# Down products of a macaron encoder as 2x2x2 block products, with the residual kept in DRAM meanwhile

## The chip, the core and the metric

The kernel runs on one core of a Trainium2 chip. The core has engines that work side by side, each on its own instructions in order: PE multiplies matrices (it loads a 128x128 weight block, then streams columns past it), DVE and ACT work on rows of 128 partitions, POOL does simple row operations and issues transfers of its own, SP only issues transfers. 16 DMA engines move the data that SP and POOL ask for. Only POOL's transfers can add to what lies at the destination. An engine waits for another on semaphores; an instruction that waits holds up all behind it on its engine.

The metric is the device time of one execution, in microseconds (us), as a median of several.

## The reference

Two layers on 528 tokens (16 meta tokens ahead of 512 frames) with 1024 features. Each layer has a feed-forward network (FFN), a mixer (attention beside a convolution), and a second FFN; so there are four FFNs. All values are float32.

```python
def swiglu(x, w_gate, w_up, w_down):
    return (jax.nn.silu(x @ w_gate) * (x @ w_up)) @ w_down
...
    for l in range(DEPTH):
        h = h + 0.5 * swiglu(rmsnorm(h, ffn1_norm[l]), ffn1_w_gate[l], ffn1_w_up[l], ffn1_w_down[l])
        h = h + hybrid_mixer(rmsnorm(h, mix_norm[l]), w_in[l], w_attn_out[l], conv_w[l], conv_b[l],
                             conv_ln_g[l], conv_ln_b[l], w_conv_out[l], w_out[l])
        h = h + 0.5 * swiglu(rmsnorm(h, ffn2_norm[l]), ffn2_w_gate[l], ffn2_w_up[l], ffn2_w_down[l])
    h = rmsnorm(h, final_norm)
    return h[:, N_META:]
```

The hidden width is 2816, which is 22 row tiles of 128. The last FFN works on the 512 frames alone.

## The kernel before

Features lie on partitions, tokens along the row: `h[0..7]` are eight tiles of 128 x 528. A float32 product is made of three products of rounded parts: each operand x is split into `hi`, a rounded copy (ACT, L79), and `lo`, the remainder (DVE, L80), and hi·hi, hi·lo and lo·hi are added up. So each weight tile and each activation passes ACT and DVE once before PE can use it.

**Weights** come in units, in the order of a list (L131 to 155). `unit` (L243) hands out the next one and prepares three units ahead: a raw tile `wr` (three buffers, loaded by SP at L191) is split into `wh` and `wl` (four buffers each). In the mixer DVE is spared: ACT writes the rounded copy and its negative (L224, L225), and a transfer from POOL adds the raw weight from DRAM to the latter (L226).

**Gate and up products** of two row tiles are made as one 2x2x2 block product in `quad` (L566): the depth is cut into two halves, the rows into two tiles, the tokens into two halves. Seven products of blocks stand for eight: four with weight blocks as they are (`w11`, `w22`, `w21` and, inside sums, `w12`), the others with sums of weight blocks, `s1` to `s4`. The sums `s1` and `s3` are made by transfers: SP loads one block, POOL adds a second from DRAM (`fetch_sums`, L196, L208 and L210, two buffers each); `s2` and `s4` follow from `s1` by a DVE addition (L236). The products run at L580 and are combined in PSUM by ACT copies and DVE operations (L599 to 613).

**Down products** (`down`, L622) run after each group of row tiles. The groups are

```python
GROUPS = ((0, 4), (4, 10), (10, 16), (16, 22))
```

For each of the eight output tiles j, in the order of `ORDER`, one unit of weights (`wr<-wd`, 384 KB for six row tiles) is multiplied with the group's split activations (L260): six row tiles x three products x two token halves, 36 matmuls of 264 columns, or 18 of 512 columns in the last FFN. For all but the last group, DVE scales the result by one half and by the norm factor (L638) into `dt`, and POOL adds that to `h[j]` in place (L640). The last group's result goes into `h[j]` directly (L633), and what the next part needs of `h[j]` is prepared there (`after`).

**Activations**: `parts` (L484) splits each row tile of silu(gate)·up into `ah` and `al`, six buffers each. `late` holds a row tile whose split is put into the next quad.

An FFN begins with plain rows (`head`, `first_head`): two row tiles, four in the first FFN, whose gate and up products are made without blocks while the sums are being built.

## Time and profile before

| what | us |
|---|---|
| median of 3 runs | 2152.22 |
| lowest, highest | 2151.51, 2152.39 |
| profiled execution: span from first to last instruction | 2150.5 |

No separate time of the profiled execution is at hand beyond its span; it lies 1.7 us under the median of the runs.

By windows of the trace, the four FFNs take 368.33, 357.56, 357.64 and 356.71 us, the two mixers 361.67 and 348.59 us.

How to read the profile's lines: a group line names the source line, the engine, the operation, what it writes and reads, and the count; then the busy time in us and the mean duration of one in ns; then the idle time of the engine before these instructions and what ended it. A line of windows gives, for a stretch in us from the start, its length, the busy time and number of instructions of each engine, PE's granted clock (1.00 is full), the share of time in which the DMA engines were taken, and what they moved in GB/s. A piece of the chain in order of time gives its start, its length, and the instructions in it. A line of a DMA queue gives packets, MB, and the time of the packets as a share of 16 engines; q1 holds SP's transfers, q0 those of POOL. A line of DMA issues ends with the size of one and the median time from issue to landing.

### The profile page before, as it was taken

Reading aid. Unit: us, or ns where it says so; the run is one execution under the profiler, and the core shown is the slowest. Engines: PE = TensorE matmul, PEld = TensorE weight load, DVE = VectorE, ACT = ScalarE, POOL = GpSimd, SP = SyncE. Lnnn points to the kernel's source line nnn. Section 1 sums busy time; section 2 is a strip of 40 time slices with the busy share of each in tenths; the row PEclk is TensorE's granted clock in tenths of the full one; section 3 lists DMA queues with packets and bytes.
Section 4 is the critical chain, followed back from the end, with each engine's and each line's share of the span. In section 5 each row is a group of like instructions: output and inputs, shape, how many; then the busy total and the mean of one; then the engine's idle time right before and its main releaser. Section 6 shows DMA issues by size and latency. Waiting matters only on the chain.

```text
span 2150.5 us, 39932 instructions
## 1 busy us (share of the span) xinstructions
PE 2135.9 (99%) x16226; PEld 2052.8 (95%) x16226; DVE 1521.5 (71%) x2091; ACT 1137.9 (53%) x1587; POOL 488.7 (23%) x449
## 2 busy tenths in 40 slices
PE   9999999999999999999999999999999999999998
PEld 9999999999999999999999999999888889999897
DVE  7867685677766777677877676856677767767685
ACT  6434355467776545343554443554778775444354
POOL 1322321211111131313113223212112111322320
PEclk9999999999999999999999999999999999999999
DMA  8465536865578747464365655368656886665542
GB/s 236 133 165 141 142 104 198 181 138 119 134 169 180 175 129 189 129 161 122 99 169 145 168 140 146 103 193 184 142 127 133 187 188 167 159 175 143 144 111 77
DMA packets 140168, 324.90 MB, mean 151 GB/s; under 512 B 15568, under 2 KB 19664, under 8 KB 139984
## 3 DMA queue, kind: packets, MB, share of 16 engines
q1 hardware_dynamic: 101856, 226.36, 33.3%
q0 software_dynamic: 37440, 95.44, 26.1%
q8 instruction: 127, 2.08, 0.4%
q10 hardware_dynamic: 688, 0.55, 0.1%
q14 instruction: 57, 0.47, 0.1%
HBM read 315.86 MB, written 6.42 MB: 150 GB/s over the span
## 4 chain that ended last, share of the span: by engine, by line
PE 99%; ACT 0%; DVE 0%; DMA 0%; issue 0%; DVEq 0%; ACTq 0%
PE pb L580 16%; PE ps L580 16%; PE ps L720 15%; PE ps L260 12%; PE ps L706 10%; PE pe L260 6%; PE pb L260 6%; PE pe L580 5%; PE z L706 2%; PE ps L502 2%; PE pe L502 1%; PE pb L502 1%; PE z L877 1%; PE po L921 1%; PE z L900 1%; PE ps L554 1%
## 5 line engine op out<-in xcount | busy, mean ns | idle before, releaser
L79 ACT CAST wh<-wr 128x1024 fp32r<-128x1024 f32 (+4 forms) x275 | 242.2, 887 | 372.4 <-PE ps L260 94.5
L80 DVE TENSOR_TENSOR wl<-wr,wh 128x1024 fp32r<-128x1024 f32 (+4 forms) x275 | 300.6, 1096 | 57.4 <-ACT wh L79 53.5
L79 ACT CAST wh<-s 128x1024 fp32r<-128x1024 f32 x158 | 165.8, 1049 | 274.9 <-DVE s L236 83.1
L80 DVE TENSOR_TENSOR wl<-s,wh 128x1024 fp32r<-128x1024 f32 x158 | 216.1, 1368 | 59.4 <-ACT wh L79 58.7
L720 PE MATMUL ps<-uh,wh 128*128 128x264 f32 (+1 forms) x792 | 243.8, 308 | 0.0
L720 PE MATMUL ps<-uh,wl 128*128 128x264 f32 (+1 forms) x792 | 240.0, 303 | 0.0
L720 PE MATMUL ps<-ul,wh 128*128 128x264 f32 (+1 forms) x792 | 239.9, 303 | 0.0
L640 POOL TENSOR_TENSOR h<-h,dt 128x528 f32<-128x528 f32 (+1 forms) x96 | 179.9, 1879 | 258.1 <-DVE dt L638 255.2
L210 POOL DMA_DIRECT2D s<-wg x78 | 72.8, 938 | 596.9 <-DMA s<-wg 337.9
L748 DVE SCALAR_TENSOR_TENSOR y<-uc,prm,y 128x528 f32<-128x528 f32 (+1 forms) x240 | 197.7, 824 | 4.1
L224 ACT CAST wh<-wr 128x1024 fp32r<-128x1024 f32 x104 | 109.1, 1049 | 141.2 <-issue 46.9
L580 PE MATMUL ps<-ul,wh 128*128 128x264 f32 (+1 forms) x624 | 177.4, 284 | 0.0
L580 PE MATMUL pb<-sl,wh 128*128 128x264 f32 (+1 forms) x624 | 176.9, 283 | 0.0
L580 PE MATMUL ps<-uh,wl 128*128 128x264 f32 (+1 forms) x624 | 176.9, 283 | 0.0
L580 PE MATMUL pb<-sh,wl 128*128 128x264 f32 (+1 forms) x624 | 176.8, 283 | 0.0
L580 PE MATMUL pb<-sh,wh 128*128 128x264 f32 (+1 forms) x624 | 176.5, 283 | 0.0
L580 PE MATMUL ps<-uh,wh 128*128 128x264 f32 (+1 forms) x624 | 176.2, 282 | 0.0
L720 PEld LDWEIGHTS ps<-uh,wl 128*128 128x128 f32 x792 | 149.1, 188 | 5.9
L720 PEld LDWEIGHTS ps<-uh,wh 128*128 128x128 f32 x792 | 148.9, 188 | 5.4
L720 PEld LDWEIGHTS ps<-ul,wh 128*128 128x128 f32 x792 | 149.0, 188 | 5.1
L260 PE MATMUL ps<-ah,wh 128*128 128x264 f32 (+1 forms) x616 | 142.0, 300 | 0.0
L260 PE MATMUL ps<-ah,wl 128*128 128x264 f32 (+1 forms) x616 | 141.8, 300 | 0.0
(319 smaller groups left out, 6460.8 us busy)
## 6 DMA issues: line engine op xcount, KB each, us to landing
wr<-wd SPq DMA_DIRECT2D x96, 384.0 KB, 3.6
wr<-win SPq DMA_DIRECT2D x72, 512.0 KB, 4.4
wl<-win POOLq DMA_DIRECT2D x72, 512.0 KB, 7.8
wr<-wg SPq DMA_DIRECT2D x117, 256.0 KB, 3.0
wr<-wu SPq DMA_DIRECT2D x117, 256.0 KB, 3.4
s<-wg SPq DMA_DIRECT2D x78, 256.0 KB, 5.2
s<-wu SPq DMA_DIRECT2D x78, 256.0 KB, 5.7
s<-wg POOLq DMA_DIRECT2D x78, 256.0 KB, 5.2
```

The costliest lines, as they stand in the source:

```text
L79: act.copy(hi, x)
L80: dve.tensor_tensor(out=lo, in0=x, in1=f(hi), op=ALU.subtract)
L210: pool.dma_start(t[:, a:b], src, accum_op=ALU.add)
L224: act.copy(hi[:, :nk], raw[:, :nk])
L260: pe.matmul(ps[:, c, :n], wt[:, k0 + k, :], xt[:, s:s + n], start=(k == 0 and pi == 0), stop=(k == end and pi == 2))
L502: pe.matmul(ps[:, e, :TH], wt[:, k, :], xt[:, s], start=(k == ORDER[0] and pi == 0), stop=(k == ORDER[-1] and pi == 2))
L554: pe.matmul(ps[:, e, :TH], wt[:, k, :], xt[:, s], start=(k == 0 and pi == 0), stop=(k == KD - 1 and pi == 2))
L580: pe.matmul(ps[:, e, :TH], wt[:, 4 * e + kk, :], xt, start=start and kk == 0 and pi == 0, stop=kk == 3 and pi == 2, skip_group_check=True)
L640: pool.tensor_tensor(out=tri(h[j], mode), in0=tri(h[j], mode), in1=tri(t, mode), op=ALU.add)
L706: pe.matmul(ps, wt[:, k0 + k, :], xt[:, s], start=(n == 0 and pi == 0), stop=(n == nk - 1 and pi == 2))
L720: pe.matmul(ps, wt[:, k, :], xt[:, s], start=(n == 0 and pi == 0), stop=(n == KD - 1 and pi == 2))
L748: t = dve.scalar_tensor_tensor(out=y, in0=uc[i][:, c0 + k:k + T], scalar=col(w0 + k), in1=y, op0=ALU.mult, op1=ALU.add)
```

## The change

Of the 22 row tiles of each FFN, the first 18 now go through block products in the down stage too. There are three groups of six row tiles and a last one of four, and the two row tiles of a quad are three apart, so that a group's first three tiles and last three are the two halves of the depth:

```diff
-GROUPS = ((0, 4), (4, 10), (10, 16), (16, 22))
-PLAIN, PLAIN_FIRST = 2, 4
+GROUPS = ((0, 6), (6, 12), (12, 18), (18, 22))
+NH = 3
+PAIRS = tuple(tuple((m0 + i, m0 + NH + i) for i in range(NH)) for m0, _ in GROUPS[:-1]) + (((18, 19), (20, 21)),)
+PLAIN, PLAIN_FIRST = 1, 2
...
+    DOWN = ((0, "w11"), (0, "w21"), (0, "s1"), (0, "s2"), (1, "w11"), (0, "s3"), (0, "w22"), (0, "s4"),
+            (1, "s1"), (1, "s2"), (1, "w21"), (1, "s3"), (1, "w22"), (1, "s4"))
```

A group's down stage is two block products, d = 0 and 1. Each makes four output tiles, two of the first four and two of the last four, for both token halves. Its seven units have 18 matmuls each, of 264 or 256 columns:

```diff
+            def down_quads(sp, gi):
+                item = late.pop()
+                sum_ops(dve, *item)
+                sum_parts(*item)
+
+                def products(ps, name, d, start=False):
+                    hi, lo = unit(name, fi, l, ("d", gi, d))
+                    for k in range(NH):
+                        xh, xl = a_parts[name, k]
+                        for pi, (wt, xt) in enumerate(((hi, xh), (hi, xl), (lo, xh))):
+                            for e in range(2):
+                                pe.matmul(ps[:, e, :TH], wt[:, NH * e + k, :], xt, start=start and k == 0 and pi == 0,
+                                          stop=k == NH - 1 and pi == 2, skip_group_check=True)
...
+                def give(src, c, t, d):
+
+                    dt = two(fp.tile([P, T], F32, tag="nt", bufs=3, name="dt"), mode)
+                    r = norm["r"][:, toks[t]].unsqueeze(1).to_broadcast([P, 2, TH])
+                    dve.scalar_tensor_tensor(out=dt, in0=src, scalar=0.5, in1=r, op0=ALU.mult, op1=ALU.mult)
+                    j = 4 * c + 2 * d
+                    pool.dma_start(residual[j:j + 2, :, toks[t]].rearrange("k p t -> p k t"), dt, accum_op=ALU.add)
...
+                A, B = begin_quad(0)
+                for d in range(2):
+                    if d == 0:
+                        products(A, "w21", 0)
+                        give(v(A), 0, 0, 0)
+                    G = ptile()
+                    products(G, "s1", d, True)
+                    q = sp.tile([P, 2, TH], F32, tag="q", bufs=2, name="q")
+                    act.copy(q, v(G))
+                    products(B, "s2", d)
+                    E = ptile("pe")
+                    dve.scalar_tensor_tensor(out=v(E), in0=v(B), scalar=-1.0, in1=q, op0=ALU.mult, op1=ALU.add)
+                    if d == 0:
+                        A = ptile()
+                        products(A, "w11", 1, True)
+                    else:
+                        products(A, "w21", 1)
+                        give(v(A), 0, 0, 1)
+                    products(B, "s3", d)
+                    c22 = sp.tile([P, 2, TH], F32, tag="c22", bufs=2, name="c22")
+                    dve.scalar_tensor_tensor(out=c22, in0=v(B), scalar=-1.0, in1=q, op0=ALU.mult, op1=ALU.add)
+                    products(E, "w22", d)
+                    give(c22, 1, 1, d)
+                    give(v(E), 1, 0, d)
+                    products(B, "s4", d)
+                    give(v(B), 0, 1, d)
+                    if d == 0:
+                        B = ptile("pb")
+                        act.copy(v(B), v(A))
```

The weights of these units: raw blocks `w11`, `w21`, `w22` of 384 KB, whose remainder is made in the way of the mixer, by a second ACT pass and an adding transfer from POOL; the sums `s1` and `s3` by transfers and `s2`, `s4` by DVE, as in a quad. The sums of the next block product are now asked for at its predecessor's `s1`, not at `w11`:

```diff
-            if nk == "w11":
+            if nk == "s1":
                 fetch_sums()
...
+            if is_down(n) and nk in RAW_OF:
+                act.copy(hi[:, :size], raw)
+                act.activation(lo[:, :size], raw, AF.Copy, scale=-1.0)
+                for a, b, src in pieces(n):
+                    pool.dma_start(into(lo, n, a, b), src.bitcast(F32R), accum_op=ALU.add)
+            else:
+                split(raw, hi[:, :size], lo[:, :size])
```

The activations need sums and differences of blocks too, and room for all their parts. Each pair of row tiles now has three and a half split rows in place of two. The four half-width operations that make the sums run on POOL inside the next quad, and for the last pair of a group on DVE ahead of the down stage:

```diff
+            def sum_ops(eng, p, ua, ub):
+
+                t1, t2 = toks
+                for o, x, y, op in ((ub[:, t2], ua[:, t2], ub[:, t2], ALU.subtract),
+                                    (ua[:, t2], ua[:, t1], ua[:, t2], ALU.subtract),
+                                    (ua[:, t1], ub[:, t2], ua[:, t1], ALU.subtract),
+                                    (ub[:, t1], ub[:, t1], ua[:, t1], ALU.add)):
+                    eng.tensor_tensor(out=o, in0=x, in1=y, op=op)
```

For that room `h` leaves the core: `leave` writes it to a DRAM tensor `hd` early in the FFN (SP, eight transfers of 264 KB), the freed tiles take activations (`slot`), `give` adds each result to `hd` by a transfer from POOL, and `back` loads `h` again ahead of the last quad.

```diff
+            def leave():
+
+                for k in ORDER:
+                    nc.sync.dma_start(tri(residual[k], mode), tri(h[k], mode))
+
+            def back():
+
+                for k in ORDER:
+                    h[k] = hpool.tile([P, T], F32, tag=f"h{k}", bufs=1, name=f"h{k}")
+                    nc.sync.dma_start(tri(h[k], mode), tri(residual[k], mode))
```

The order of instructions on two engines shows what moves. First POOL, in the first FFN. Before, this is what stands there around the down stage of the second group: the sums of the next quad, then the eight additions into `h`, then again sums.

```order
L210 DMA s3_2077<-wg1 128x512
L210 DMA s3_2077<-wu1 128x512
L210 DMA s1_2072<-wg1 128x512
L210 DMA s1_2072<-wu1 128x512
L640 TENSOR_TENSOR h0_77<-h0_77,dt_1922 128x528
L640 TENSOR_TENSOR h4_81<-h4_81,dt_1925 128x528
L640 TENSOR_TENSOR h1_78<-h1_78,dt_1972 128x528
L640 TENSOR_TENSOR h5_82<-h5_82,dt_2019 128x528
```

Now, in the same group's down stage, only transfers stand there: remainders of raw blocks (`wl<-wd`, L263), additions into the residual (`hd<-dt`, L747), and the next quad's sums (`s1`, `s3`, L230).

```order
L263 DMA wl_2303<-wd1 128x2x384
L747 DMA hd_134<-dt_2327 128x2x264
L263 DMA wl_2356<-wd1 128x2x384
L230 DMA s3_2416<-wg1 128x512
L230 DMA s3_2416<-wu1 128x512
L230 DMA s1_2411<-wg1 128x512
L230 DMA s1_2411<-wu1 128x512
L747 DMA hd_134<-dt_2466 128x2x264
L747 DMA hd_134<-dt_2469 128x2x264
L263 DMA wl_2473<-wd1 128x2x384
L747 DMA hd_134<-dt_2495 128x2x264
L263 DMA wl_2526<-wd1 128x2x384
```

The remainder `wl_2473` (of `w21` of the second block product) stands behind the next quad's four sum transfers and two additions into the residual; before, no weight of the down stage passed POOL.

Second ACT, at the same place. Before, one rounded copy per unit of down weights, between the last activations of the group:

```order
L79 CAST wh_1799<-wr_1698 128x768
L103 ACTIVATE g_1592<-g_1592 128x264
L79 CAST ah_1795<-up_1594 128x528
L79 CAST wh_1836<-wr_1731 128x768
L103 ACTIVATE g_1591<-g_1591 128x264
L79 CAST ah_1832<-up_1593 128x528
L79 CAST wh_1842<-wr_1763 128x768
```

Now the raw blocks have two passes each (L260, then L261), with copies out of PSUM (`pb`, `q`) and splits of activation sums (`ap`) between them:

```order
L260 CAST wh_2302<-wr_2152 128x768
L753 COPY pb_2300<-ps_2276 128x2x264
L261 ACTIVATE wl_2303<-wr_2152 128x768
L81 CAST ap_2272<-up_2010 128x528
L81 CAST ap_2268<-up_2011 128x528
L81 CAST wh_2331<-s3_1937 128x768
L260 CAST wh_2355<-wr_2115 128x768
L764 COPY q_2353<-ps_2330 128x528
L261 ACTIVATE wl_2356<-wr_2115 128x768
```

The pass that a POOL transfer waits for (`wl_2303`) comes behind a copy that waits for PE's first product of the stage (`ps_2276`).

More of the change, by code (lines that the diff above doesn't have):

```diff
@@ L174 @@
         if nk == "w11":
-            fetches += [n, n + 5, n + 3]
+            place = {units[x][2]: x for x in range(n, min(n + len(DOWN), len(units))) if units[x][0][1:] == key[1:]}
+            early = is_down(n) and key[3][2] == 0
+            fetches += [place[x] for x in (("w11", "w21", "w22") if early else ("w11", "w22", "w21"))]
         elif nk not in QUAD:
@@ L603, in quad @@
                 act.copy(q, v(G))
-                while late:
-                    parts(*late.pop())
+                for item in late:
+                    if last:
+                        parts(*item)
+                    else:
+                        sum_ops(pool, *item)
+                if last:
+                    late.clear()
                 products(B, "s2", sx(1))
```

157 lines of the change are left out of this document (106 added, 51 removed).

## The prediction

> **What bounds the kernel now.** I read the page first: busy times, the slices, the chain that ended last.
>
> ```profile
> PE 2135.9 (99%) x16226; PEld 2052.8 (95%) x16226; DVE 1521.5 (71%) x2091; ACT 1137.9 (53%) x1587; POOL 488.7 (23%) x449
> DMA  8465536865578747464365655368656886665542
> DMA packets 140168, 324.90 MB, mean 151 GB/s; under 512 B 15568, under 2 KB 19664, under 8 KB 139984
> q1 hardware_dynamic: 101856, 226.36, 33.3%
> q0 software_dynamic: 37440, 95.44, 26.1%
> PE 99%; ACT 0%; DVE 0%; DMA 0%; issue 0%; DVEq 0%; ACTq 0%
> ```
>
> The chain is PE from end to end, so a matmul that goes is worth its full slot, as long as nothing else becomes late. The second resource to watch is in the lower rows: the 16 DMA engines are already about 60% taken (33.3 + 26.1), with no wait on them in the chain. I then asked for windows: three 2x2x2 quads, the down stage behind them, the stage of the mixer with the densest transfers, and each feed-forward (FFN) as a whole.
>
> ```profile
> core 0: us, PE busy (x) PEld busy (x) DVE busy (x) ACT busy (x) POOL busy (x), PEclk, DMA share, GB/s
> 175.47:236.93 61.46, 61.46 (x506) 61.46 (x506) 45.89 (x60) 30.94 (x44) 11.86 (x13) 1.00 0.68 172
> 236.93:271.87 34.94, 34.94 (x291) 34.94 (x290) 19.52 (x21) 8.42 (x11) 14.02 (x7) 1.00 0.36 106
> 368.33:409.65 41.32, 41.32 (x343) 41.32 (x342) 23.27 (x36) 19.92 (x24) 10.43 (x13) 1.00 0.87 199
> 1052.41:1087.56 35.15, 35.15 (x291) 35.15 (x290) 30.19 (x48) 23.59 (x37) 1.92 (x2) 1.00 0.38 118
> ```
>
> One cycle of an FFN is three quads and a down stage: 61.46 + 34.94 = 96.4 us, with the DMA engines taken for 0.68 x 61.46 + 0.36 x 34.94 = 54.4 us of it. Even at a share of 0.87 (third row) PE doesn't stop.
>
> **What the change removes.** The pieces of the chain in order of time give the price of a matmul:
>
> ```profile
> 175.47 5.84 PE ps L580 x48
> 236.93 8.74 PE ps L260 x72
> 2011.53 8.38 PE ps L260 x36
> 2044.93 5.70 PE ps L580 x48
> ```
>
> 121.7 ns in a quad, 121.4 ns in a down stage, in the last FFN 232.8 ns for 512 columns and 118.8 ns for 256. A down stage of six row tiles has 8 x 6 x 3 x 2 = 288 matmuls (35.0 us); the two block products have 2 x 7 x 18 = 252 (30.7 us): 4.3 us less, in nine stages 38.6 us. In the last FFN 144 x 232.8 ns = 33.5 us becomes 252 x 118.8 ns = 29.9 us: 3.6 us, three times, 10.8 us. In all **49.4 us**, if PE stays the bound: a span of 2101.1 us. The regrouping costs nothing by itself (the same quads and plain rows, and again 22 row tiles).
>
> **What it adds: DMA work.** By the code, a stage had 8 loads of 384 KB. It now has 10 (six raw blocks, four first halves of sums), and on POOL's queue 10 adding transfers of 384 KB (four sums, six remainders) and 8 adding transfers of 264 KB into the residual. Prices come from the queue rows of two narrow windows in which almost only adding transfers ran (first 195.4 to 199.4 us, 2-KB packets; then 386 to 389 us, 4-KB packets), and from q1 above:
>
> ```profile
> q0 software_dynamic: 278, 0.51, 87.6%
> ...
> q0 software_dynamic: 115, 0.43, 77.5%
> ```
>
> 0.51 MB took 87.6% of 4.0 us, 146 GB/s, 225 ns a packet; 0.43 MB took 77.5% of 3.0 us, 185 GB/s, 354 ns a packet. Plain loads: 226.36 MB in 33.3% of 2150.5 us, 316 GB/s, so 1.24 us for 384 KB. The new adding transfers have shorter runs: 1536 bytes (256 packets, 16 on each engine) and 1056 bytes. No row shows these, nor adding into DRAM. From one side, only bytes count: at 146 GB/s 2.7 us and 1.85 us. From the other, a packet costs 225 ns whatever its size: 3.6 us each. A line through the two rows gives 193 ns and 162 ns, so 3.1 us and 2.6 us, and I take these: 1536 lies near the 2-KB row. Cheaper than by bytes is excluded as long as shorter packets aren't faster.
>
> Row first, then a rule: two adding transfers took 3.5 us of all engines above. The Trainium skill, "DMA: Bandwidth & Descriptors", section "Anatomy of one DMA — SWDGE (gpsimd) path", fits such a transfer as 2.0 us plus its bytes at 436 GB/s; that would be 1.2 us for the same bytes, and an estimate by it of 9.0 + 5.0 us for a stage's 10 and 8 transfers, which would hide all of it (the third rival's result). The rows show a third of that rate for transfers that add. The same page, "Specifications", puts line rate at 512 bytes and up, which would be the end by bytes; between the two packet sizes here the rate differs by 27%, so I don't rest on it.
>
> The sum for a cycle: three quads 54.4 - 8 x 1.24 = 44.5 us, loads 12.4, sums and remainders 31.0, residual 20.8: **108.7 us of all 16 engines**, beside 61.5 + 30.7 = 92.2 us of PE. The engines can't be over 100% taken, so a cycle lacks 16.5 us. There are eight such cycles. In the first cycle of FFNs two to four a plain pair stands for a quad (four units of 512 KB, 6.6 us, beside 23.4 us of PE) and the residual is written out (2.16 MB, 6.8 us): 107.3 against 95.1, 12.2 us short; in the first FFN, with two plain pairs, about 1 us. 8 x 16.5 + 3 x 12.2 + 1 = 170 us. Not all of it stops PE: three buffers of differences (nt) let the last three additions of a stage run on, and behind the third stage of each FFN comes the last group, with a cheap down stage and engines to spare: 4 x 3 x 2.6 = 31 us off. Waits added: **139 us**. With the prices by bytes (each cycle 10.0 us less) it is 37 us, with those by packets (13.0 us more) about 283. I count a taken share of 100%; 0.95 in its place would add some 65 us.
>
> **Where it waits.** A remainder (wl) now comes by two ACT passes and a POOL transfer, and its buffer comes free four units ahead of use, so three units of 18 matmuls cover it, 3 x 2.19 = 6.6 us (17.5 us in the mixer, where the same way is in use).
>
> ```profile
> L225 ACT ACTIVATE wl<-wr 128x1024 fp32r<-128x1024 f32 x104 | 109.5, 1053 | 0.0
> L79 ACT CAST wh<-wr 128x768 fp32r<-128x768 f32 x96 | 79.1, 836 | 162.1 <-PE ps L260 48.9 <-issue 38.8 <-PE pe L260 27.9
> L226 POOL DMA_DIRECT2D wl<-win x72 | 62.1, 863 | 332.8 <-ACT wl L225 221.5 <-ACT e L103 41.0 <-DVE y L748 32.2
> wl<-win POOLq DMA_DIRECT2D x72, 512.0 KB, 7.8
> s<-wg POOLq DMA_DIRECT2D x78, 256.0 KB, 5.2
> s<-wu POOLq DMA_DIRECT2D x78, 256.0 KB, 7.2
> ```
>
> Two passes of 0.84 us, 0.3 us to POOL, and a landing between 5.2 and 7.8 us, say 6.5: 8.5 us. That is 1.9 us late, twice a stage (for w11 and w21 of the second block product; the units between get the same delay for cover): 3.9 us, 46 us in 12 stages, even with idle engines. It lies inside the 139 us, not on top: the DMA queue's delay is the same wait, longer. On POOL's queue, in order, these remainders stand behind the next quad's four sum transfers and three residual additions, at 0.86 us and more each; a blocked POOL holds SP's loads only through full buffers, but PE through the remainder.
>
> **What I cost at nothing.** DVE in a down stage, from the rows below and those of 768 columns:
>
> ```profile
> L80 DVE TENSOR_TENSOR wl<-wr,wh 128x768 fp32r<-128x768 f32 x96 | 95.8, 997 | 9.9 <-ACT wh L79 8.7
> L236 DVE TENSOR_TENSOR s<-s,wr 128x1024 f32<-128x1024 f32 x78 | 112.4, 1441 | 0.9
> L638 DVE SCALAR_TENSOR_TENSOR dt<-ps,rstd 128x528 f32<-128x528 f32 x36 | 25.3, 706 | 70.3 <-PE ps L260 69.0 <-POOL h L640 1.3
> ```
>
> 8 splits x 1.0, 4 sums x 1.08 (three quarters of 1441 ns), and 8 results, 4 combinations, 4 half-width sums and 2 splits of activations at 0.71 at most: 25.1 of 30.7 us. ACT, 20 passes x 0.84 and some copies, 20 us. Both fit; if their order doesn't, up to 2 us a stage, 24 us. POOL's additions into h go; nothing waited for them. Loading h back is 2.16 MB beside the last quad. The last down stage shrinks to 23.3 us: in the window from 1052.41, DVE's 30.19 us less a third of its 8 splits is 27.5, so it becomes the later one by up to 5 us, once.
>
> **The sum.** 2150.5 - 49.4 + 139 = 2240 us of span. The median of the runs is 2152.22, 1.7 us more than the profiled span; rounded, I say **2240 us**.
>
> **Rivals.**
> 1. *Only the start of the remainders is late*, engines never full: 2150.5 - 49.4 + 46 = 2147, with landings of 7.8 us 2178; 2149 to 2180 us as a time. For it: 0.87 of the engines without a stop. Against: 108.7 us don't go into 92.2. Chance 0.20.
> 2. *A packet costs the same at any size*: 283 us of waits, about 2385, up to 2430 with queues. For it: 2-KB packets move at 146 GB/s where 4-KB ones reach 185. Against: the line through them still falls. Chance 0.16.
> 3. *All hidden, faster*: PE stays the bound, 2103 us, to 2125 with small waits. One mechanism decides it, the rate of adding transfers with short runs: 92.2 - 44.5 - 12.4 = 35.3 us are left for 6.1 MB, so above 172 GB/s, with a landing under 4.6 us. For it: 185 GB/s in one row; against: that row has the longest packets. Chance 0.14.
> That the change saves no matmul time is excluded by the counts above.
>
> **How the numbers follow.** The forecast, DMA engines full, 2185 to 2330 us, has 0.50. The range leaves out rival 3 and the upper part of rival 2: 2125 to 2385 us. A measurement of this kernel can tell about 0.2% (4.3 us). Faster by more: rival 3 and a quarter of rival 1, 0.19; within: 0.05; slower: 0.76.
>
> **What would show it.** PE's matmuls fall by 324 in three FFNs and rise by 312 in the last, so that 16214 are left; their count says little, their gaps all. Right: DMA digits of 9 through the FFNs, a share over 0.9 in the down stages, PE gaps of 8 to 20 us a stage that end with a DMA into wl, landings there over 8 us. Wrong: PE at 99% again (rival 3), or gaps of 2 us twice a stage with shares under 0.85 (rival 1). Adding transfers into DRAM that cost far from 2.6 us would break the sum.

## The result and the profile after

| kernel | median, us | lowest to highest | runs | ratio to before, 95% interval |
|---|---|---|---|---|
| before | 2151.89 | 2151.51 to 2152.39 | 4 | |
| changed | 2352.18 | 2346.34 to 2356.26 | 4 | 1.093, 1.0912 to 1.0948 |

The changed kernel is 9.3% slower, 112 us above the forecast and inside its range. The page of its profile (span 2353.3 us), in the same rows as before: busy times, the granted clock and the DMA share in 40 slices, transfers, queues, and the chain by engine.

```profile
PE 2163.2 (92%) x16214; PEld 2076.6 (88%) x16214; DVE 1619.4 (69%) x2307; ACT 1299.6 (55%) x1851; POOL 684.6 (29%) x657
PEclk9899999999999999999999999999999999999999
DMA  8789795965578779889578897959756786979792
DMA packets 226961, 424.54 MB, mean 180 GB/s; under 512 B 20432, under 2 KB 110544, under 8 KB 226768
q0 software_dynamic: 96192, 168.39, 43.3%
q1 hardware_dynamic: 129888, 252.97, 34.8%
PE 25%; DMA 5%; DVE 2%; issue 1%; ACT 1%; POOL 0%; POOLq 0%; SPq 0%; DVEq 0%; ACTq 0%
```

The remainders and the residual additions in the view of transfers, with the median time from issue to landing at the end:

```profile
wl<-wd POOLq DMA_DIRECT2D x72, 384.0 KB, 8.3
hd<-dt POOLq DMA_DIRECT2D x72, 264.0 KB, 7.7
```

PE now has 190.1 us without work (2353.3 - 2163.2; before 14.6). What it waits for, from the view of waits (us in total, times, longest):

```profile
PE ps L735 <- DMA wl<-wd: 91.8, 36, 9.7
PE pe L735 <- DMA wl<-wd: 47.3, 12, 4.6
PE pb L670 <- DVE pe L703: 15.5, 11, 1.7
PE pe L437 <- ACT nt L81: 5.1, 1, 5.1
```

The first two rows are the down products' remainders: 139.1 us in 48 waits, three to five in each of the twelve down stages. But PE's busy time rose too, by 27.3 us (2135.9 before), although 49.4 us of matmul time were to go. Windows of 2 us around one wait show where that came from; the last columns are the granted clock of PE, the DMA share and GB/s.

```profile
210.00:212.00 2.00, 2.00 (x17) 1.84 (x16) 1.89 (x3) 0.05 (x1) 0.86 (x1) 1.00 0.93 237
212.00:214.00 2.00, 0.05 (x1) 0.00 (x0) 1.97 (x4) 0.83 (x1) 0.00 (x0) 1.00 1.10 251
214.00:216.00 2.00, 0.63 (x3) 0.66 (x4) 0.26 (x1) 0.00 (x0) 0.12 (x1) 0.65 1.10 258
216.00:218.00 2.00, 2.00 (x11) 2.00 (x11) 0.00 (x0) 0.00 (x0) 0.92 (x2) 0.50 1.06 174
218.00:220.00 2.00, 2.00 (x11) 2.00 (x11) 1.18 (x2) 1.57 (x2) 2.00 (x3) 0.50 0.88 127
220.00:222.00 2.00, 2.00 (x13) 2.00 (x13) 0.40 (x1) 0.01 (x1) 2.00 (x2) 0.65 1.08 129
222.00:224.00 2.00, 2.00 (x19) 2.00 (x18) 1.62 (x2) 1.42 (x2) 1.16 (x2) 1.00 0.90 179
```

After a wait of 3.3 us PE's clock is at 0.50: 11 matmuls in 2 us where 19 fit once it is back. The trace shows 27 such stretches at 0.50 while PE works, 146.8 us in all. PE is busy in 115.0 us of them, so half of that, **57.5 us**, is lost. (The mean clock of the run, 0.968, can't be used for this: it also counts the parts of these stretches in which PE stands still.) Before, no half clock fell on PE's work. The account of the span: +202.8 = **-30.2 us of matmuls at full clock (2135.9 to 2163.2 - 57.5) + 175.5 more idle + 57.5 of half clock**.

Of the 48 waits, 25 are of 3.05 us or more, and each of these has a stretch at 0.50 that begins in it or just behind it; the other 23, up to 1.88 us, have none. The two stretches left belong to a wait of 5.1 us elsewhere and to two short ones in a row (1.2 and 1.4 us).

Where in a cycle the waits stand, from the timeline of PE (start, length, instruction, and in brackets the idle time before it and what ended it), in one down stage (two block products of seven units):

```profile
201.11 0.51 PE L735 MATMUL ps<-ap,wl 128*128 128x264 f32 x2 [1.34 <-DMA wl<-wd]
207.40 0.51 PE L735 MATMUL ps<-ap,wl 128*128 128x264 f32 x2 [0.67 <-DMA wl<-wd]
215.37 0.78 PE L735 MATMUL pe<-ap,wl 128*128 128x264 f32 x2 [3.32 <-DMA wl<-wd]
231.47 0.67 PE L735 MATMUL ps<-ap,wl 128*128 128x264 f32 x2 [4.42 <-DMA wl<-wd]
```

These are w21 of the first product, w11 of the second, w22 of the first (into `pe`) and w21 of the second. And the DMA share around them, in windows over the stage, the quad behind it, and one whole cycle:

```profile
188.00:196.00 8.00, 8.00 (x67) 7.94 (x66) 5.42 (x10) 5.38 (x10) 3.67 (x3) 1.00 1.02 213
196.00:204.00 8.00, 6.65 (x51) 6.22 (x51) 6.51 (x13) 5.01 (x8) 1.20 (x1) 1.00 1.00 199
...
228.00:236.00 8.00, 4.54 (x24) 4.54 (x25) 1.43 (x3) 1.04 (x1) 1.96 (x3) 0.79 1.13 272
...
252.00:262.00 10.00, 10.00 (x84) 10.00 (x83) 7.86 (x12) 4.54 (x7) 3.53 (x4) 1.00 1.03 259
262.00:300.00 38.00, 36.70 (x302) 36.48 (x301) 31.27 (x41) 22.04 (x33) 16.04 (x12) 1.00 0.58 139
201.11:305.34 104.23, 94.32 (x729) 93.23 (x729) 69.70 (x90) 49.00 (x70) 42.59 (x38) 0.95 0.88 194
```

The engines are full from 188 us on, through the stage and the first quad behind it (no window of 8 us there is under 0.95), and at 0.58 after it. The share adds up the times of packets and can pass 1: over 188 to 262 us it is 1.05. Over the whole cycle it is 0.88: 91.7 us of engine time in 104.2 us.

### The profile page after: what moved, and what is told of

The parts are those of the page before. It is cut to its first block, busy times and chain, and to the rows that moved or that the text cites. A ratio compares the mean times of both kernels' runs of the same rounds, so it can differ in the third digit from the quotient of the medians.

```text
span 2353.3 us, 41120 instructions
## 1 busy us (share of the span) xinstructions
PE 2163.2 (92%) x16214; PEld 2076.6 (88%) x16214; DVE 1619.4 (69%) x2307; ACT 1299.6 (55%) x1851; POOL 684.6 (29%) x657
## 3 DMA queue, kind: packets, MB, share of 16 engines
q0 software_dynamic: 96192, 168.39, 43.3%
q1 hardware_dynamic: 129888, 252.97, 34.8%
## 5 line engine op out<-in xcount | busy, mean ns | idle before, releaser
L81 ACT CAST wh<-s 128x1024 fp32r<-128x1024 f32 (+1 forms) x254 | 246.0, 969 | 279.2 <-issue 91.7
L82 DVE TENSOR_TENSOR wl<-s,wh 128x1024 fp32r<-128x1024 f32 (+1 forms) x254 | 301.3, 1186 | 57.0 <-ACT wh L81 55.9
L81 ACT CAST wh<-wr 128x1024 fp32r<-128x1024 f32 (+3 forms) x179 | 162.6, 913 | 223.0 <-PE ps L735 68.0
L82 DVE TENSOR_TENSOR wl<-wr,wh 128x1024 fp32r<-128x1024 f32 (+3 forms) x179 | 192.8, 1081 | 35.5 <-ACT wh L81 34.2
L670 PE MATMUL pb<-sh,wh 128*128 128x264 f32 (+1 forms) x624 | 178.5, 286 | 17.0 <-DVE pe L703 15.5
L735 PE MATMUL ps<-ap,wl 128*128 128x264 f32 (+1 forms) x432 | 99.0, 318 | 93.2 <-DMA wl<-wd 91.8
L230 POOL DMA_DIRECT2D s<-wg x78 | 75.6, 971 | 333.3 <-DMA s<-wg 215.4
L561 POOL TENSOR_TENSOR up<-up 128x264 f32<-128x264 f32 (+1 forms) x96 | 127.1, 1324 | 149.5 <-DVE up L684 97.1
L735 PEld LDWEIGHTS ps<-ap,wl 128*128 128x128 f32 x432 | 73.9, 211 | 101.7 <-DMA wl<-wd 96.5
L747 POOL DMA_DIRECT2D hd<-dt x96 | 129.8, 1506 | 91.9 <-DVE dt L745 87.6
L246 POOL DMA_DIRECT2D wl<-win x72 | 61.9, 859 | 320.6 <-ACT wl L245 195.2
L735 PE MATMUL pb<-ap,wh 128*128 128x264 f32 (+1 forms) x864 | 155.0, 304 | 0.0
```

The lines of the kernel that those rows point to most:

```text
L81: act.copy(hi, x)
L82: dve.tensor_tensor(out=lo, in0=x, in1=f(hi), op=ALU.subtract)
L230: pool.dma_start(into(t, n, a, b), src, accum_op=ALU.add)
L246: pool.dma_start(lo[:, :nk], src[:, :nk].bitcast(F32R), accum_op=ALU.add)
L561: eng.tensor_tensor(out=o, in0=x, in1=y, op=op)
L670: pe.matmul(ps[:, e, :TH], wt[:, 4 * e + kk, :], xt, start=start and kk == 0 and pi == 0, stop=kk == 3 and pi == 2, skip_group_check=True)
```

## The experiments

In the quoted expectations ScalarE is ACT, VectorE DVE, GpSimd POOL, SyncE SP and TensorE PE. All medians, beside runs of the kernel before of 2151.4 to 2152.0 us:

| kernel | median, us | ratio, 95% interval | granted clock | waits for wl<-wd, us |
|---|---|---|---|---|
| changed | 2352.18 | 1.0912 to 1.0948 | 0.968 | 139.1 |
| e1_dve_remainder | 2252.29 | 1.0451 to 1.0486 | 0.980 | 0 |
| e2_no_give | 2325.35 | 1.0785 to 1.0828 | 0.972 | 114.7 |
| e4_neither | 2181.79 | 1.0119 to 1.0160 | 0.990 | 0 |
| e6_plain_lo | 2308.91 | 1.0703 to 1.0745 | 0.973 | 116.8 |
| e13_no_quad_sums | 2326.99 | 1.0794 to 1.0823 | 0.975 | 110.2 |
| e12_sums_late | 2403.47 | 1.1156 to 1.1189 | 0.959 | 184.2 |
| e5_lo_first | 2354.27 | 1.0917 to 1.0955 | 0.967 | 140.0 |
| e8_two_ahead | 2375.60 | 1.1028 to 1.1061 | 0.961 | 177.3 |
| e16_lo_first | 2378.64 | 1.1031 to 1.1089 | 0.962 | 149.6 |
| e17_one_ahead | 2357.22 | 1.0937 to 1.0970 | 0.967 | 138.0 |
| e18_both | 2351.84 | 1.0908 to 1.0952 | 0.966 | 138.4 |
| e3_fill | 2377.82 | 1.1035 to 1.1073 | 0.980 | 75.8 |
| e10_gap_short | 2337.43 | 1.0848 to 1.0884 | 0.972 | |
| e11_gap_long | 2278.83 | 1.0575 to 1.0606 | 0.975 | |
| e14_gap_mini | 2296.30 | 1.0657 to 1.0685 | 0.974 | |
| e7_six_dt | 2199.81 | 1.0212 to 1.0246 | 0.986 | 0 |
| e9_back_late | 2157.94 | 1.0018 to 1.0037 | 0.996 | 0 |
| e15_sum_first | 2163.30 | 1.0039 to 1.0063 | 0.995 | 0 |

### Which of the added transfers PE waits for: e1, e2, e4

e1 makes the down products' remainders on DVE from the raw tile, as the kernel before did:

```diff
-            if is_down(n) and nk in RAW_OF:
+            if False:
```

e2 leaves out the residual additions of the second and third group (64 of 96), so the residual lacks their results; e4 does both.

```diff
-                    pool.dma_start(residual[j:j + 2, ...], dt, accum_op=ALU.add)
+                    if gi == 0:
+                        pool.dma_start(residual[j:j + 2, ...], dt, accum_op=ALU.add)
```

> Remainders of the raw down blocks are made by DVE again, not by adding transfers (72 transfers of 384 KB less). Theory (PE's waits are the landings of these transfers, and the halved PE clock follows from the waits): the 139 us that PE waits for wl<-wd go, the granted clock is back above 0.99, and the span falls by 139 + 70 to about 2145 us. Rival (DVE takes over as the bound: 25.1 + 6 = 31 us of work in a stage of 30.7 us): new waits on DVE's wl of 60 to 100 us, 2190 to 2250 us.

> 64 of the 96 adding transfers into the residual are left out (those of the second and third group of each FFN), so those groups' results are missing; the remainders still come by transfers. Theory (the DMA engines are full in the down stages, so the remainders land late): waits for wl<-wd fall from 139 us to under 90, the clock's loss halves, 2230 to 2290 us. Rival (the chain of two ACT passes, POOL and a landing is too long even with idle engines): waits stay above 115 us, 2320 to 2345 us.

> Remainders by DVE, and the 64 adding transfers into the residual left out (the results of two groups are missing). If the DMA engines bound the change, this is its time without them: 2105 to 2125 us, with under 20 us of waits. If DVE is the next bound, it equals the run with remainders by DVE to within 10 us.

e1 is 100 us faster than the changed kernel. Its time is at the upper end of its rival's range, but not for the rival's reason: the 139 us are gone, 33 us of half clock are left, and the new waits are not for DVE's remainders but mostly for the additions. Its waits of PE:

```profile
PE pb L670 <- ACT pb L689: 53.7, 14, 5.9
PE pb L670 <- DVE pe L703: 15.5, 11, 1.7
PE pb L735 <- DVE c L776: 12.1, 8, 3.7
```

The first row is a copy that needs the bank `pb`, whose last reader on DVE stands behind one that waits for a `dt` buffer; DVE's own wait for `hd<-dt` is 114.7 us in 44 waits. e2 alone gains only 27 us, close to what its rival said (whose reason, too long a chain, the next runs test): the remainders still come late with two thirds of the additions gone. Together they gain 170 us, more than 100 + 27, since with the remainders off PE's path the additions are what it waits for next. Even so e4's 2182 us fits neither of its two theories; PE's longest sums of waits there are 16.9 us behind ACT's copies into `pb` and 15.5 us behind DVE's E. The queue rows, of e1 and then e2, also give prices:

```profile
q0 software_dynamic: 76608, 140.08, 37.9%
...
q0 software_dynamic: 78784, 151.22, 38.8%
```

Against the changed kernel, q0's time falls by 43.3% x 2353.3 - 37.9% x 2249.0 = 167 us for e1's 72 remainders, **2.3 us each** of all 16 engines, and by 119 us for e2's 64 additions (38.8% of 2320.1 us left), **1.9 us each**.

### Why the remainders land late: e5, e6, e8, e12, e13, e16 to e18

Three theories: the remainder's own chain (buffer, two ACT passes, issue, landing) is longer than the look-ahead; adding is what takes long; or full engines, where the transfers around it set the time.

```diff
 e5:
-                act.copy(hi[:, :size], raw)
                 act.activation(lo[:, :size], raw, AF.Copy, scale=-1.0)
+                act.copy(hi[:, :size], raw)
 e6:
-                    pool.dma_start(into(lo, n, a, b), src.bitcast(F32R), accum_op=ALU.add)
+                    pool.dma_start(into(lo, n, a, b), src.bitcast(F32R))
 e8 (AHEAD = ((0, "w22"), (1, "w21"))) and e17 (AHEAD = ((0, "w22"),)), at the end of prep_unit:
+        n += 2
+        if n < len(units) and is_down(n) and (units[n][0][3][2], units[n][2]) in AHEAD:
+            ahead[n] = quads["pool"].tile([P, 2 * NH, P], F32R, tag="wa", bufs=1, name="wa")
+            remainder(n, ahead[n])
 e12, in fetch_sums, with state["late"] the last remainder's transfer:
+                    tc.add_manual_dep(i.ins, state["late"].ins.name, NOSYNC, reason="behind the remainder")
 e12, and in prep_unit the second product's s1 no longer calls fetch_sums, its w21 does so at its end:
+            if nk == "w21" and second:
+                fetch_sums()
 e13:
-            for a, b, src in pieces(n, "w12"):
+            for a, b, src in pieces(n, "w12") if is_down(n) or not is_down(n - 1) else ():
 e16 (and e18, with e17's part):
-                act.copy(hi[:, :size], raw)
-                act.activation(lo[:, :size], raw, AF.Copy, scale=-1.0)
+                i = act.activation(lo[:, :size], raw, AF.Copy, scale=-1.0)
+                tc.add_manual_dep(act.copy(hi[:, :size], raw).ins, i.ins.name, NOSYNC, reason="remainder first")
```

> The two passes of ScalarE ahead of each down product's remainder change places: the negated copy (840 ns) first, the plain cast (835 ns) behind it, so that each of the 72 remainder transfers can be issued 0.84 us earlier. Theory 'late start' (landing is measured from the issue, the 3-product look-ahead is too short for the chain of copy, issue and landing): 48 waits lose up to 0.84 us each, 40 us, and the clock gives back about as much again times 0.4: 2290 to 2325 us. Rival 'full engines' (the transfers end when their bytes have moved, whenever they were issued): 2345 to 2356, waits for wl<-wd still above 130 us.

> The remainder transfers of the down products write instead of add (the weights' remainders are then wrong; same bytes read from DRAM, same 256 runs, same issue order). If adding itself is what makes a landing long, the landing falls from 8.2 us to about 5 us and the waits for wl<-wd from 139 us to under 70: 2230 to 2285 us. If it is the position of the issue and the company on the 16 engines, landing stays at 7 to 8.5 us and the time at 2330 to 2356.

> Of the changed kernel: the remainders of w22 of the first product of a stage and of w21 of the second (the two with the longest waits in the timeline, 3.3 and 4.4 us) get a buffer of their own and are issued two products (4.4 us of PE) earlier; q and c22 have one buffer instead of two to make room. Theory 'late start': the 47.3 us of waits on pe and about half of the 91.8 on ps go, 80 to 95 us, and with them 30 to 55 us of half clock: 2205 to 2245. Rival 'full engines': the other remainders come as much later as these come earlier: 2320 to 2356.

e5 was no edit on the chip: the scheduler kept the order of the two passes, so its 2354 us is the changed kernel measured once more. e6 gains 43 us and lies between its two theories: landing 7.0 us instead of 8.3, waits 116.8 us instead of 139.1. Adding is about a fifth of the matter. q0's time falls by 70 us for the 72 transfers (41.1% of 2309.1 us left): 1.0 us of the 2.3 us is the adding. e8 lost 23 us, worse than both its theories: the early w22 landed in 5.2 us and was not waited for, but the second w21, which took the same buffer, was held by it, issued in a crowd, and came 16.1 us later.

> The changed kernel with the four adding transfers of the next quad's sums (s from wg and wu, 256 KB each) behind the remainder of the second w21 on GpSimd's queue instead of ahead of it. Theory (that remainder is late because these four and the residual additions share the engines just then, 10.8 us from issue to landing): its nine waits of some 4.4 us fall under 1.5 us, 25 to 40 us less waiting on wl<-wd and 10 to 20 us less of half clock; up to 10 us come back where the next quad waits for its sums: 2295 to 2335. Rival (the remainder is late by its own chain, or the engines are full through the whole stage): 2345 to 2360, waits for wl<-wd 130 us or more.

> The changed kernel without the four adding transfers of the sums of the quad that follows each down stage (48 transfers of 256 KB in all; those quads then compute with unsummed weights). e12 moved these four behind one remainder, and the remainder then behind them came 17.4 us after its issue. Theory (a remainder is late when other adding transfers stand ahead of it in the queue of GpSimd's transfers): the waits of the second product's remainders go, 50 to 90 of the 139 us on wl<-wd, and 20 to 45 us of half clock with them: 2220 to 2280. Rival (each remainder is late by its own 8 us, whoever stands ahead): waits above 115 us, 2320 to 2350.

e12 moved the crowd and came out slower than both its theories. The second w21 is then waited for 3.1 us instead of 4.4 in the stage shown, but the second w22, now behind the four sums, was issued at 227.65 us and came 17.4 us later, 7.8 us of them a wait; in all 45 us more of waits. e13 took the sums away and saved 29 us of waits, less than either end of what its theory said and near its rival: the company in the queue matters, and is not most of it.

> What e5 was meant to be: in e5's trace ScalarE still makes the plain cast first and the negated copy behind it, since the scheduler orders the two passes itself, so e5 was the changed kernel again. Here the cast is tied behind the copy. In after the copy starts 0.74 to 1.27 us behind the start of the cast, so each remainder can be issued 0.7 to 1.2 us earlier. Theory 'late start' (a remainder's own chain of buffer, copy, issue and some 8 us of landing is longer than the look-ahead): 48 waits shorten by up to that, 35 to 50 us, half clock falls by some 15 to 25 us: 2280 to 2310. Rival (the arrival is set by the transfers that stand ahead): 2340 to 2356.

> As e8, but only the remainder of w22 of the first product has the extra buffer and the two products' earlier issue (in e8 it landed in 5.2 us and was not waited for; the other one, which took the same buffer, was held until that was free and took 16.1 us). q and c22 with one buffer as in e8. Theory 'late start': its waits, most of the 47.3 us on pe, go, and 15 to 25 us of half clock: 2275 to 2305. Rival (full engines, the others come later by as much): 2335 to 2360.

> e16 and e17 together. Theory 'late start': the two gains add up, waits for wl<-wd at 50 to 70 us, 2215 to 2250. Rival (full engines): 2330 to 2360. If e16 and e17 gain and e18 gains no more than the better of them, the engines set a floor behind the chain.

e17 and e18 fall on their rival's side; e16 is 26 us slower than the changed kernel, which neither theory said. e17's waits:

```profile
PE ps L747 <- DMA wl<-wd: 137.1, 37, 10.0
...
PE pe L747 <- DMA wl<-wd: 0.9, 4, 0.3
```

The waits on `pe` fell from 47.3 to 0.9 us, as the early issue should do, and the sum is still 138 us. The timeline of that stage:

```profile
204.25 0.51 PE L747 MATMUL ps<-ap,wl 128*128 128x264 f32 x2 [0.39 <-DMA wl<-wd]
226.79 0.81 PE L747 MATMUL ps<-ap,wl 128*128 128x264 f32 x2 [9.13 <-DMA wl<-wd]
```

What PE doesn't wait at w22 it waits at w21 of the second product: 9.13 us instead of 4.42. (In e8, e17 and e18 `q` and `c22` have one buffer instead of two; the new waits for `c`, 6.2 to 7.0 us, are small beside this.)

The landings decide against the late start. In each of the twelve stages POOL issues the same nine transfers in a row: four sums of the next quad, three residual additions, and the remainders of the second w21 and w22. From the first issue to the last they take 16.5 us in the changed kernel (median of the stages), 15.5 in e16, 8.0 in e17, 7.3 in e18 and 5.3 in e8. From the first landing to the last they take 20.0, 21.4, 18.7, 19.0 and 18.8 us. The second w21 of the stage shown is issued at 220.58 us in the changed kernel and lands after 10.8 us; in e17 it is issued at 212.50 and lands after 14.3. So the stage's transfers land at a pace that earlier issue hardly changes, and PE takes the rest as waiting, at one place or another. The sum of the waits is no constant: other orders raised it, to 149.6 us in e16, 177.3 in e8 and 184.2 in e12. What sets the pace in detail (bytes, packets, the adding, the order in the queue) stays open: e2, e6 and e13 each take 22 to 29 us of waits off with 70 to 119 us of engine time, and only e1, which takes 167 us and the wait's object, takes them all.

### What a wait costs beside itself: e3, e10, e11, e14

e3 puts 816 extra matmuls of 240 columns ahead of the remainders' products, into unused columns of their banks (which changes these products' results), so that PE works where it waited. e10 forces 24 gaps into the kernel before by a matmul on a tile that passes ACT and POOL first, e11 12 longer ones, e14 24 with an earlier start; the added matmul writes beside the block product `B` in its bank, which changes that product's result.

```diff
 e3, FILL = {(1, "w11"): 8, (0, "w22"): 24, (1, "w21"): 36}:
+                                for r in range(FILL.get((d, name), 0)):
+                                    pe.matmul(ps[:, r % 2, 512 - 240:], hi[:, 0, :], xh[:, :240], ...)
 e10 (every quad but a group's last; e11 every second and four passes; e14 with E in place of B):
+                    act.copy(z[:, :TH], B[:, 1, :TH])
+                    pool.tensor_tensor(out=z[:, :TH], in0=f(z[:, :TH]), in1=f(z[:, :TH]), op=ALU.subtract)
+                    state["gap"] = pe.matmul(B[:, 0, 384:], z[:, :P], z[:, :P], ...)
```

> 68 matmuls without use per down stage (240 columns, about 0.11 us each, 7.5 us a stage, 90 us in all) stand ahead of the three remainders that PE waits for longest. Theory (the clock is halved because PE stands still): PE works in its waits, the granted clock rises from 0.968 to above 0.99, and the span falls by 50 to 76 us to 2275 to 2305 us although PE does more. Rival (the clock falls for another reason, such as transfers or load): the clock stays at 0.97, the span stays at 2353 or rises by up to 20 us.

e3 fits neither theory: the clock rose to 0.980 and the time to 2378 us. In the profiled executions the fillers cost 92.7 us of PE time at full clock (2233.2 us busy less 34.8 of half clock, against 2105.7), PE's idle time falls by 50.3 us (waits for remainders by 63.3, but copies into `pb` come late by 16 us more), and half clock falls by 22.7 us: 19.7 us more in all, as the spans show. Filling waits gives back part of the clock and costs more than it gives.

> The kernel before with 24 forced gaps of TensorE at the ends of quads: a dummy matmul that reads a tile that ScalarE and one GpSimd pass wrote, and that the following products stand behind. Each gap should be about 2 us, 24 of them 45 to 55 us. Both theories: time = 2152 plus the idle time of TensorE that the trace shows, if gaps of 2 us leave the granted clock alone (theory: it is the single gap's length that halves the clock): 2195 to 2210, granted clock still 0.99 or more. Rival (the clock follows the idle share, about 0.4 us lost for each us idle, as after against before suggests): 2215 to 2230.

> As e10, but 12 gaps, each with four GpSimd passes instead of one, 4 to 5 us: about the same idle time in all. Theory (a gap of over some 3.5 us costs 3.4 or 6.8 us at half clock, so 1.7 to 3.4 us on top of the gap): 20 to 41 us more than idle time alone explains, 2225 to 2250, granted clock 0.98 to 0.99. Rival (clock follows the idle share): the same time as e10 within 10 us, if the idle times agree.

> As e10 (24 forced gaps, one GpSimd pass each), but the chain starts one product earlier, so that the gaps should be some 2.9 us shorter than e10's 5.6 us: 2 to 3.5 us, 50 to 80 us in all. Theory (a gap's length decides: below some 3 us the clock stays): time less idle time within 10 us of before's 2136 us of busy TensorE, so 2205 to 2235. Rival (every forced gap costs some 2.1 us of busy time more, as in e10): 51 us more, 2255 to 2285.

The gaps came out longer than meant, since ACT's and POOL's queues stand ahead of the chain. PE's busy time and waits of e10, then e11, then e14:

```profile
PE 2187.3 (94%) x16250; PEld 2099.1 (90%) x16250; DVE 1523.3 (65%) x2091; ACT 1146.4 (49%) x1611; POOL 510.6 (22%) x473
...
PE pb L628 <- POOL z L627: 134.1, 24, 7.2
```

```profile
PE 2167.1 (95%) x16238; PEld 2081.4 (91%) x16238; DVE 1523.8 (67%) x2091; ACT 1142.2 (50%) x1599; POOL 526.3 (23%) x497
...
PE pb L628 <- POOL z L627: 96.1, 12, 9.5
```

```profile
PE 2188.4 (95%) x16250; PEld 2100.8 (92%) x16250; DVE 1522.6 (66%) x2091; ACT 1145.1 (50%) x1611; POOL 516.1 (22%) x473
...
PE pb L628 <- DVE up L596: 49.2, 11, 4.8
PE pb L628 <- POOL z L627: 43.3, 13, 3.5
```

Against 2135.9 us of busy PE before: 51.4 us more for 24 gaps of 5.6 us on average, 31.2 us more for 12 gaps of 8.0 us, 52.5 us more for 24 gaps of 3.3 to 4.5 us. So a gap costs **2.1, 2.6 and 2.2 us on top of itself**, nearly the same for 3.3 as for 8 us. By idle time it would be 0.38, 0.32 and 0.57 us for each us: the price goes by the gap. The changed kernel has the same price, 57.5 us for 27 stretches, 2.1 us each. The extra cost is what e11's theory and e14's rival said, though all three times missed their ranges, since the gaps were longer than planned; e14's were too long to test its own theory.

The waits of all traces test it. Counted are waits with PE at work for 3.5 us on either side, in the changed kernel and the experiments, without their last 40 us. Half clock follows all 229 waits of 3.5 us or more, 47 of 54 from 3.0 to 3.5 us, 35 of 73 from 1.9 to 3.0 us, and 11 of 280 from 1.0 to 1.9 us. So the length decides, but the threshold isn't sharp.

### Can the rest be repaired: e7, e9, e15

e7 is e1 with every second `dt` in a buffer of `g`. e9 adds to it that the residual's loads back (`back`, L523) stand behind the next weight loads on SP's queue. e15 adds to that DVE's E ahead of the parts' passes, and the norm's passes ahead of the block sums.

```diff
 e7:
-                    dt = two(fp.tile([P, T], F32, tag="nt", bufs=3, name="dt"), mode)
+                    dt = two(gtile() if state["dt"] % 2 else fp.tile([P, T], F32, tag="nt", bufs=3, name="dt"), mode)
 e9, back() called from inside the last quad, ahead of its w21:
-                    nc.sync.dma_start(tri(h[k], mode), tri(residual[k], mode))
+                    i = nc.sync.dma_start(tri(h[k], mode), tri(residual[k], mode))
+                    tc.add_manual_dep(i.ins, state["load"].ins.name, NOSYNC, reason="behind the weights")
 e15, in whole_part, with behind = the instruction that makes E:
+                    tc.add_manual_dep(i.ins, behind.ins.name, NOSYNC, reason="behind the sum product")
```

> e1_dve_remainder (2252.3) with every second residual tile dt in the buffers of g, so that six buffers instead of three are open to residual additions in flight. Theory: e1's 53.7 us of waits for pb are copies behind a VectorE instruction that waits for a dt buffer, so these fall under 15 us, and the clock gives back some 15 to 25 us: 2180 to 2205. Rival (the additions take as long as they take, and the queue only holds more of them, or the g buffers are needed by the next quad's gating): 2235 to 2255.

> e7_six_dt (2199.8) with the eight loads of the residual back into SBUF put behind the next quads' weight loads on SyncE's queue. In e7 seven of them hold the queue for 16 us from 306.5 us on, and four waits of 8 to 10 us (37.5 us in all, one in each feed-forward pass) stand behind them. Theory: these four waits go and some 13 us of half clock with them: 2140 to 2165, so at or below the kernel before. Rival (the residual then comes late for the last group's additions, or the weight loads were late by themselves because the engines are full): 2185 to 2210.

> e9_back_late (2157.9) with VectorE's E = q - B of a quad ahead of the two passes over the parts of the pair before, which wait for ScalarE while E is ready, and with the norm's passes of a feed-forward pass ahead of the block sums. Theory: the 15.5 us of waits for pe (11 of 1.4 us) go, and up to 5 us more for the norm: 2136 to 2147, faster than the kernel before by 0.2 to 0.7%. Rival (the passes then come late for the down products): 2150 to 2160.

e7 gains 52 us on e1. Its largest wait left is 37.5 us in six waits for `pb`, nearly all in four of 8.2 to 9.8 us, one in each FFN behind the third down stage. SP's queue there (start, time to issue, instructions):

```profile
305.90 0.43 SPq L211 DMA_DIRECT2D wr<-wu  x1
306.49 16.06 SPq L523 DMA_DIRECT2D h<-hd  x7
322.65 0.37 SPq L211 DMA_DIRECT2D wr<-wg  x1
```

Seven loads of the residual wait 16 us, and the next weights stand behind them; DVE waits 8.8 us for those, PE 9.1. With the loads behind the weights, e9 loses all four waits:

```profile
196.00:204.00 8.00, 8.00 (x67) 8.00 (x67) 5.79 (x8) 3.80 (x5) 3.78 (x4) 1.00 1.00 198
204.00:212.00 8.00, 8.00 (x68) 8.00 (x67) 6.09 (x8) 3.37 (x4) 3.11 (x4) 1.00 1.13 296
212.00:220.00 8.00, 8.00 (x68) 8.00 (x67) 6.58 (x7) 3.91 (x6) 5.42 (x5) 1.00 1.13 250
```

PE doesn't stop in the stage although the DMA engines are as full as in the changed kernel: what fills them now are loads for the next quads, sums, and additions that PE doesn't wait for. The busy times of e9:

```profile
PE 2104.7 (98%) x16214; PEld 2027.7 (94%) x16214; DVE 1671.8 (78%) x2379; ACT 1247.4 (58%) x1779; POOL 594.1 (28%) x585
```

e9 stands at 1.0027, 0.3% above the kernel before, with 31 us less of busy PE and 32 us more of idle time (46.8). e15 shortened the waits for `pe` from 15.5 to 8.7 us but brought up 12.3 us of others, and is 5 us slower than e9, outside both its ranges. No kernel here beats the one before.

## Why the prediction was wrong in size

The forecast's span was 2240.1 us, the measured one 2353.3. The 113.2 us between them are 57.5 of half clock, 36.4 of other waits, and 19.2 of a saving that came out smaller (rounded).

- **The term that failed: what a microsecond of waiting costs.** The sum was "2150.5 - 49.4 + 139 = 2240 us of span", with PE's clock at full. The waits for remainders were 139.1 us, but the 25 longer ones of them, of 3.05 us or more, each halved the clock. Half clock adds 57.5 us, 2.1 us for each of 27 stretches; forced gaps measure 2.1 to 2.6 us. The forecast spoke of gaps of 8 to 20 us a stage and left this out. The Trainium skill, "TensorE: Matmul & The Clock Gate", Part 1, has a rule for it in "The HAM clock gate": the clock is halved after at least one idle window of about 3.4 us, and comes back after about 3.4 us of work. The traces agree in the stretches, 13 of 3.4 us, 12 of 6.8 and 2 of 10.2; but 35 of 73 waits of 1.9 to 3.0 us halved the clock too. In the section "HAM oscillation" the same page of the Trainium skill tells of a like case, waits for DMA that cross the window each time.
- **The saving** came out smaller. The matmuls are 16214, as forecast, but PE's busy time at full clock is 2163.2 - 57.5 = 2105.7 us, where the forecast had 2135.9 - 49.4 = 2086.5: 30.2 us saved, not 49.4. e9, which hardly waits, agrees: at a clock of 0.996 at most 8.6 us of its 2104.7 us can be half clock, so it saves 31 to 40 us. Where the rest goes stays open. A part are restarts: the pair of matmuls behind the wait of 1.34 us is recorded at 0.51 us, later pairs at 0.41.
- **Other waits**, 36.4 us (175.5 - 139.1). The part on "what I cost at nothing" allowed up to 24 us if the order of DVE and ACT doesn't fit; 15.5 us are DVE's late E, and the rest are small. Of the same part, "loading h back is 2.16 MB beside the last quad" was covered only because PE waited elsewhere: once the remainders and `dt` were repaired it cost four waits, 36.7 us.
- **The DMA prices** were too high: 3.1 us for a remainder (2.3 measured), 2.6 us for an addition (1.9, the forecast's own end by bytes). A cycle took 91.7 us of engine time, not 108.7, so "a cycle lacks 16.5 us" was false on the average. And a share can pass 100% in this measure (1.05 over 74 us), which the forecast excluded. By the measured prices the forecast's sum gives 37 us of waits or fewer, and a time at or under the kernel before. That it gave 139, and 139.1 was measured, is luck, two errors against each other: the average of a cycle hides that the engines are full in the stage and the first quad (0.95 to 1.13) and at 0.58 in the other quads. That the look-ahead of three units can't move work from the one into the other is likely by the code, but no run tests it by itself.
- **Where it waits** was right in object (wl, 11.6 us a stage on average, landings over 8 us) and wrong in a part of the reason. The chain of 8.5 us against 6.6 us of cover was to give 46 of the 139 us; e16, e17 and e18 start remainders earlier and gain nothing. Waiting on POOL's order costs little (the issue at 220.58 us follows ACT's pass, done at 220.01, by 0.6 us); what stands ahead in the queue counts (e12, e13), as the forecast said, for some 29 us.
- **The rivals.** The first (late start alone) is out by e18. The second, a packet price, is out by the prices, though its time is closest: right size, other cause. The third needed adding transfers above 172 GB/s and a landing under 4.6 us; the remainders moved at about 170 (0.393 MB in 2.3 us), the additions at about 145 (0.270 MB in 1.86 us), and the remainders landed in 8.3. e9 shows that the block products can come to par, once DVE makes the remainders.

## What to carry to other kernels

Compare DMA time with compute time stage by stage, not over a cycle: a transfer that PE needs soon gets late as soon as its own stage fills the engines, while in e9 engines as full (1.00 to 1.13) cost PE nothing, since it waited for none of these transfers. Price each PE wait of 3 us or more at itself plus about 2 us of half clock (from 2 to 3 us about every second one), and count waits, not only their sum. Take half clock from PE's busy time inside its stretches, not from the mean clock. When a wait is repaired, look at what it covered: here two more stood behind the first, and taking them away gave 52 and 42 us.

## What the runs showed of the hardware that was not expected

- The price of a gap barely depends on its length: 2.2 us for 3.3 to 4.5 us (means), 2.1 for 5.6, 2.6 for 8.0. Whether a gap of 1.9 to 3.0 us costs it is open each time: 35 of 73 did.
- Adding cost 1.0 us of all 16 engines for 384 KB (2.3 against 1.3 us), and little latency: landing 8.3 against 7.0 us.
- Earlier issue doesn't mean earlier arrival of the whole: nine transfers of POOL's queue landed over 18.7 to 20.0 us whether they were issued over 5.3 us (e8), 8.0 (e17) or 16.5 (the changed kernel).
